# Taking a batched matrix product's last store out of the hand-written section and issuing one load from another engine

One core of a Trainium2 chip runs the kernel. The metric is the device time of one execution in microseconds (us), the median of several; lower is better. Spans, instruction times and DMA packets come from one profiled execution of each kernel.

## The reference

Sixteen products of 512x512 float32 matrices, the second of each transposed:

```python
batch, m, k, n = 16, 512, 512, 512
np.matmul(a, b.transpose(0, 2, 1)).astype(np.float32)   # a: 16x512x512, b: 16x512x512
```

It reads 33.55 MB and writes 16.78 MB.

## The kernel before

The kernel is written by hand, with its own semaphores (counters that one engine or transfer raises and an engine waits for), inside one section of the framework (a block that the framework enters and leaves as a whole, with a handshake of the engines). Inputs come as 16 loads of 2 MB (load 2u holds two matrices of `a`, load 2u+1 two of `b`) into 7 slots; outputs leave as 16 stores of 1 MB. DVE (VectorE) casts a load to bf16, PE (TensorE) transposes and multiplies, ACT (ScalarE) copies the product into one of 7 output slots. SP (SyncE) issues all loads but the second and stores 8 to 15; GpSimd (POOL in the profile) issues stores 0 to 7 and waits for stores to land, which frees the output slots.

```python
STORES = "SSSSOSOSOSSOOOOOO"          # what GpSimd does in turn: S issue a store, O wait for one
LATE = {11: (8, 9), 13: (10, 11), 15: (12, 13)}
# ... (semaphores and buffers cut)
load(0)                                # on SP
load(1, nc.scalar)
for n in range(2, NL):                 # NL = 7: loads 2 to 6, on SP
    load(n)
for n in range(2 * pairs):             # SP: wait for load n, tell DVE, issue load n + 6
    nc.sync.wait_ge(s_ld[n % NL], 16 * (n // NL + 1)).then_inc(s_go, 1)
    if n > 0 and n + NL - 1 < 2 * pairs:
        load(n + NL - 1)
    for m in LATE.get(n, ()):
        store(m)
store(batch - 2)
store(batch - 1)
for n in range(batch - NO, batch - 1): # stores 9 to 14 have landed
    nc.sync.wait_ge(*landed(n))

nc.gpsimd.wait_ge(s_ld[0], 32)         # GpSimd: no store before load 7 is in
for what in STORES:
    ...                                # S: store(n_st);  O: wait for landed(n_of), count s_of up
# ... (DVE, ACT and PE loops cut), then, behind that section, a second one:
with tc.tile_critical(no_gpsimd_drain=True):
    nc.sync.wait_ge(*landed(batch - 1))   # store 15 has landed
```

## Time and profile before

| | before |
|---|---|
| time, median of 3 runs | 125.49 us (125.47 to 125.68) |
| profiled span | 123.5 us |
| DMA engines, mean rate over the span | 407 GB/s |
| PE busy | 90.7 us (73%) |
| landing of the last store to the end of the span | 1.33 us |

The landing is the last of 16 arrivals at the store's semaphore, one from each DMA engine (122.217 us, in a span of 123.549 us). The profile's slices, rates, GpSimd issues and the waits of SP's queue are shown in the prediction below. These are the last two rows of the timeline; the columns are start, length, engine, line, operation, and the number of instructions merged into the row:

```profile
112.38 1.09 ACT L213 COPY ob<-ps 128x512 f32 x2 [0.60 <-PE ps L255]
113.50 0.33 SPq L109 DMA_DIRECT2D out_dram<-ob  x1
```

The last product is copied out at 113.47 us and store 15 is issued at once; nothing computes in the ten microseconds that follow. The DMA engines have a backlog of stores to work off, and then the program has to notice that they are done.

### The profile page before, as it was taken

Reading aid. Unit: us, or ns where it says so; the run is one execution under the profiler, and the core shown is the slowest. Engines: PE = TensorE matmul, PEld = TensorE weight load, DVE = VectorE, ACT = ScalarE, POOL = GpSimd, SP = SyncE. Lnnn points to the kernel's source line nnn. Section 1 sums busy time; section 2 is a strip of 40 time slices with the busy share of each in tenths; the row PEclk is TensorE's granted clock in tenths of the full one; section 3 lists DMA queues with packets and bytes.
Section 4 is the critical chain, followed back from the end, with each engine's and each line's share of the span. In section 5 each row is a group of like instructions: output and inputs, shape, how many; then the busy total and the mean of one; then the engine's idle time right before and its main releaser. Section 6 shows DMA issues by size and latency. Waiting matters only on the chain. (4 is left out here: it accounts for less than half of the span.)

```text
span 123.5 us, 2364 instructions
## 1 busy us (share of the span) xinstructions
PE 90.7 (73%) x768; PEld 55.8 (45%) x768; DVE 67.9 (55%) x96; ACT 68.1 (55%) x130; POOL 5.9 (5%) x14
## 2 busy tenths in 40 slices
PE   0000089999899999989998999899999946994000
PEld 0000079546734774476467447644764535441000
DVE  0000597891898389568928991894787078400000
ACT  4000063458946885595769558937876069555000
POOL 2000000000000160001010230000000000000000
PEclk9999999999999999999999999999999999999955
DMA  4999999999999999999999999999999999999990
GB/s 127 419 446 435 424 424 430 424 424 424 430 430 435 424 403 385 461 390 427 454 400 454 424 414 454 411 432 446 416 438 419 416 427 422 430 424 427 430 385 11
DMA packets 4608, 50.33 MB, mean 407 GB/s; under 512 B 512, under 2 KB 512, under 8 KB 512
## 3 DMA queue, kind: packets, MB, share of 16 engines
q1 hardware_dynamic: 3312, 39.85, 76.2%
q0 software_dynamic: 1152, 8.39, 16.1%
q10 hardware_dynamic: 144, 2.10, 4.3%
HBM read 33.55 MB, written 16.78 MB: 407 GB/s over the span
## 5 line engine op out<-in xcount | busy, mean ns | idle before, releaser
L255 PE MATMUL ps<-tb,ta 128*128 128x512 bf16 x256 | 57.8, 379 | 0.5
L213 ACT COPY ob<-ps 128x512 f32 x64 | 34.5, 588 | 28.5 <-PE ps L255 24.6
L195 ACT COPY ta<-tp 128x512 bf16<-128x512 bf16 x64 | 32.8, 610 | 15.4 <-PE tp L236 15.4
L255 PEld LDWEIGHTS ps<-tb,ta 128*128 128x128 bf16 x256 | 24.1, 97 | 30.7 <-issue 4.0
L236 PE MATMUL tp<-ident,ha 128*128 128x128 bf16 x256 | 19.6, 230 | 19.3 <-PEq L141 19.3
L236 PEld LDWEIGHTS tp<-ident,ha 128*128 128x128 bf16 x256 | 16.6, 103 | 23.1 <-issue 21.3
L176 DVE COPY tb<-tp 128x1024 bf16<-128x1024 bf16 x32 | 21.2, 684 | 4.8 <-DVEq L141 4.8
L236 PE MATMUL tp<-ident,hb 128*128 128x128 bf16 x256 | 18.1, 227 | 2.2 <-PEq L141 2.2
L236 PEld LDWEIGHTS tp<-ident,hb 128*128 128x128 bf16 x256 | 16.1, 102 | 2.6 <-issue 2.6
L160 DVE CAST ha<-ld 128x1024 bf16 x8 | 5.5, 686 | 13.7 <-DVEq L141 13.7
L171 DVE COPY ha<-wa 128x2048 bf16<-128x2048 bf16 x8 | 5.5, 692 | 13.6 <-DVEq L141 13.6
L166 DVE CAST wa<-ld 128x2048 bf16 x8 | 9.8, 1227 | 0.0
L166 DVE CAST wb<-ld 128x2048 bf16 x8 | 9.7, 1218 | 0.0
L160 DVE CAST hb<-ld 128x1024 bf16 x8 | 5.5, 688 | 6.4 <-DVEq L141 6.4
L109 POOL DMA_DIRECT2D out_dram<-ob x8 | 5.2, 655 | 65.2 <-DMA ld<-in_b_dram 41.1
L175 DVE COPY hb<-wb 128x2048 bf16<-128x2048 bf16 x8 | 5.5, 684 | 0.1
L163 DVE CAST ha<-ld 128x1024 bf16 x8 | 5.5, 686 | 0.0
L163 DVE CAST hb<-ld 128x1024 bf16 x8 | 5.5, 683 | 0.0
L186 ACT ACT_TABLE_LOAD x1 | 1.3, 1283 | 1.5 <-SPq L44 1.5
L80 POOL TENSOR_SCALAR_AFFINE_SELECT ident<-ident 128x128 bf16<-128x128 bf16 x1 | 0.3, 282 | 0.2 <-POOL ident L78 0.2
L78 POOL MEMSET ident<- 128x128 bf16 x1 | 0.2, 204 | 0.5 <-SPq L44 0.5
L186 ACT COPY one<-const-float32-1.0 128x1 f32<-128x1 f32 x1 | 0.2, 191 | 0.0
(4 smaller groups left out, 0.4 us busy)
## 6 DMA issues: line engine op xcount, KB each, us to landing
ld<-in_a_dram SPq DMA_DIRECT2D x8, 2048.0 KB, 26.3
ld<-in_b_dram SPq DMA_DIRECT2D x7, 2048.0 KB, 29.8
out_dram<-ob POOLq DMA_DIRECT2D x8, 1024.0 KB, 29.0
out_dram<-ob SPq DMA_DIRECT2D x8, 1024.0 KB, 19.6
ld<-in_b_dram ACTq DMA_DIRECT2D x1, 2048.0 KB, 12.2
```

The costliest lines, as they stand in the source:

```text
L109: engine.dma_start(out[n].rearrange("(p j) n -> p j n", j=J), ob[:, n % NO]).then_inc(landed(n)[0], 16)
L160: nc.vector.tensor_copy(out=h[:, :J, :], in_=src[:, :J, :HK]).then_inc(s_cd, 1)
L163: nc.vector.tensor_copy(out=h[:, J:, :], in_=src[:, J:, :HK]).then_inc(s_c, 1)
L166: nc.vector.tensor_copy(out=w[:], in_=src[:, :, HK:]).then_inc(s_w, 1)
L171: nc.vector.tensor_copy(out=ha[:], in_=wa[:]).then_inc(s_ca, 1)
L175: nc.vector.tensor_copy(out=hb[:], in_=wb[:]).then_inc(s_cb, 1)
L176: nc.vector.tensor_copy(out=tb[:, ko, :], in_=tp[:, 2 + ko % 2].rearrange("k j p -> k (j p)"),).then_inc(s_eb, 1)
L186: nc.scalar.copy(out=one[:], in_=nc.const_aps.tensor(1.0, (P, 1), f32))
L195: c = nc.scalar.copy(out=ta[:, ko, e * J * P:(e + 1) * J * P].rearrange("k (j p h) -> k j p h", j=J, h=2), in_=tp[:, ko % 2, :, e * HP:(e ...
L213: c = nc.scalar.copy(out=dst[:, j, :].rearrange("m (p j) -> m p j", j=2 * J), in_=ps[:, j, :].rearrange("m (j p) -> m p j", j=2 * J),)
L236: t = nc.tensor.transpose(tp[:, 2 * x + g, j, :], h[:, j, g * P:(g + 1) * P], ident[:])
L255: t = nc.tensor.matmul(ps[:, j, :], ta[:, ko, (e * J + j) * P:(e * J + j + 1) * P], tb[:, ko, :].rearrange("k (j p) -> k j p", j=2 * J)[:, ...
```

## The change

It has two parts. The last store leaves the hand-written section: it becomes a plain DMA of the framework behind it, which the framework itself waits for, and the waits for stores 9 to 14 go to ACT, beside that store. The closing section that did nothing but wait is gone from SP's path. And load 6, the seventh, moves from SP to GpSimd, where it waits for load 4 and comes ahead of the stores; it has its own semaphore, so `came(n)` replaces the count of arrivals.

```diff
+        def came(n):
+            if n == NL - 1:
+                return s_sw, 16
+            return s_ld[n % NL], 16 * (n // NL + (n % NL < NL - 1))
...
-        for n in range(2, NL):
+        for n in range(2, NL - 1):
             load(n)
...
         store(batch - 2)
-        store(batch - 1)
-        for n in range(batch - NO, batch - 1):
-            nc.sync.wait_ge(*landed(n))
+        nc.gpsimd.wait_ge(s_ld[NL - 3], 16)
+        load(NL - 1, nc.gpsimd)
         n_st = n_of = 0
         nc.gpsimd.wait_ge(s_ld[0], 32)
...
-    with tc.tile_critical(no_gpsimd_drain=True):
-        nc.sync.wait_ge(*landed(batch - 1))
+    with tc.tile_critical(sync_engine=act, no_gpsimd_drain=True):
+        for n in range(batch - NO, batch - 1):
+            nc.scalar.wait_ge(*landed(n))
+    waits = nc.cur_bb.bb.instructions[-1]
+    last = nc.sync.dma_start(
+        out[batch - 1].rearrange("(p j) n -> p j n", j=J), ob[:, (batch - 1) % NO]
+    )
+    tc.add_manual_dep(last.ins, waits.name, ..., reason="order of issue")   # orders, does not wait
```

(The counts in `landed` follow `came`; cut.)

More of the change, by code (lines that the diff above doesn't have):

```diff
@@ L58 @@
         s_ld = [sem(f"s_ld{i}") for i in range(NL)]
+        s_sw = sem("s_sw")
         s_st = [sem(f"s_st{i}") for i in range(SW)]
@@ L95, in load @@
                 nc.sync.wait_ge(s_cd, n - NL + 2)
-            engine.dma_start(ld[:, slot], src).then_inc(s_ld[slot], 16)
+            engine.dma_start(ld[:, slot], src).then_inc(came(n)[0], 16)
         def landed(n):
@@ L103, in landed @@
             slot = (n - STORES.count("S") + 2) % NL
-            return s_ld[slot], 16 * (len(range(slot, 2 * pairs, NL)) + 1 + (n - STORES.count("S") >= NL))
+            return s_ld[slot], came(2 * pairs - 1 - (2 * pairs - 1 - slot) % NL)[1] + 16 * (
+                1 + (n - STORES.count("S") >= NL)
+            )
         def store(n):
@@ L114 @@
         load(1, nc.scalar)
-        for n in range(2, NL):
+        for n in range(2, NL - 1):
             load(n)
         for n in range(2 * pairs):
-            nc.sync.wait_ge(s_ld[n % NL], 16 * (n // NL + 1)).then_inc(s_go, 1)
+            nc.sync.wait_ge(*came(n)).then_inc(s_go, 1)
             if n > 0 and n + NL - 1 < 2 * pairs:
@@ L265 @@
                                 t.then_inc(s_mm, 1)
-    with tc.tile_critical(no_gpsimd_drain=True):
-        nc.sync.wait_ge(*landed(batch - 1))
+    with tc.tile_critical(sync_engine=act, no_gpsimd_drain=True):
[4 more added lines that the diff above has]
+        out[batch - 1].rearrange("(p j) n -> p j n", j=J), ob[:, (batch - 1) % NO]
+    )
+    tc.add_manual_dep(
+        last.ins,
+        waits.name,
+        mybir.DependencyInfo(mybir.DependencyClass.NoSync, mybir.DependencyReason.DATA),
+        reason="order of issue",
+    )
 _INS = ['a', 'b']
```

## The prediction

> **What bounds the kernel now.** I read the page's slices first, then the DMA queues, the bytes moved by stretch, the waits of SP's queue, and last the instructions of the final 10 us one by one. One core does 16 products of 512x512; 33.55 MB come in and 16.78 MB go out.
>
> ```profile
> PE   0000089999899999989998999899999946994000
> DMA  4999999999999999999999999999999999999990
> GB/s 127 419 446 435 424 424 430 424 424 424 430 430 435 424 403 385 461 390 427 454 400 454 424 414 454 411 432 446 416 438 419 416 427 422 430 424 427 430 385 11
> ```
>
> A digit is a fortieth of the span, 3.09 us. The DMA engines read 9 in every slice from the second to the last but one, while PE starts only in the sixth and stops three slices before the end. So the kernel is bound by moving 50.33 MB at about 428 GB/s, 117.6 us, plus what lies before the first packet and after the last.
>
> ```profile
> core 0: us, PE busy (x) PEld busy (x) DVE busy (x) ACT busy (x) POOL busy (x), PEclk, DMA share, GB/s
> 12.00:42.00 30.00, 25.61 (x211) 16.98 (x212) 21.71 (x30) 16.86 (x33) 0.00 (x0) 1.00 1.01 430
> 42.00:44.00 2.00, 1.52 (x25) 1.22 (x23) 1.77 (x3) 2.00 (x5) 1.19 (x2) 1.00 1.06 451
> 44.00:46.00 2.00, 1.99 (x28) 1.65 (x28) 1.50 (x4) 1.91 (x4) 1.28 (x3) 1.00 1.08 426
> 46.00:48.00 2.00, 1.94 (x10) 0.77 (x9) 2.00 (x4) 0.79 (x2) 0.00 (x0) 1.00 0.92 332
> 48.00:54.00 6.00, 6.00 (x50) 3.53 (x49) 3.45 (x5) 4.12 (x9) 0.00 (x0) 1.00 0.98 418
> 54.00:56.00 2.00, 1.51 (x25) 1.22 (x23) 2.00 (x4) 2.00 (x5) 0.27 (x1) 1.00 1.06 438
> 56.00:96.00 40.00, 38.29 (x328) 22.78 (x326) 29.38 (x42) 28.59 (x55) 2.47 (x4) 1.00 1.01 429
> 114.00:120.00 6.00, 0.00 (x0) 0.00 (x0) 0.00 (x0) 0.00 (x0) 0.00 (x0) 0.79 1.01 427
> 120.00:122.00 2.00, 0.00 (x0) 0.00 (x0) 0.00 (x0) 0.00 (x0) 0.00 (x0) 0.50 0.12 49
> ```
>
> The last column is the rate. It is flat at 427 to 430 with one dent, from 42 to 56 us: 451x2 + 426x2 + 332x2 + 418x6 + 438x2 = 5802 there, where 14 us at 429 would be 6006, so 204/429 = 0.48 us of transfer is lost. The dent sits where GpSimd issues its first DMAs:
>
> ```profile
> 42.81 2.47 POOL L109 DMA_DIRECT2D out_dram<-ob  x4 [41.13 <-DMA ld<-in_b_dram]
> 55.73 0.53 POOL L109 DMA_DIRECT2D out_dram<-ob  x1 [10.45 <-DMA out_dram<-ob]
> ```
>
> In the DMA packets of the trace the loads' 16 KB packets, elsewhere 611 ns each, take 613 to 1099 ns from 45.0 to 47.5 us, and the first packet of GpSimd's queue starts at 47.03, 4.2 us after its issue. The stores issued there at 55.7, 63.0 and 70.4 leave no dent of that size. So it looks like a one-off price of the first use of that queue; whether of the first use, or of four stores issued together, the trace does not tell.
>
> At the end, SP waits:
>
> ```profile
> SPq L127 <- DMA out_dram<-ob: 5.8, 3, 2.4
> SPq L109 <- ACT ob L213: 1.8, 1, 1.8
> SPq L295 <- DMA out_dram<-ob: 1.7, 1, 1.7
> ```
>
> L127 are the waits for stores 9 to 14, L295 is that for store 15. By the instruction records SP issues store 15 at 113.50; the last wait of L127 ends at 119.77; a handshake between the engines takes SP from 119.96 to 120.54; the wait for store 15 ends at 122.24. Its last packet ends at 121.75, though 15 of the 16 DMA engines are done by 120.67 or so: one lags by some 1.2 us. After 122.24 SP goes through a branch (122.28), a semaphore (122.43), a drain (122.52), a no-op (122.59) and two drains (122.63 and 122.70); then two barriers of all engines end the span at 123.55.
>
> **What the Trainium skill says.** "DMA: Bandwidth & Descriptors", section "Issuing engines are not separate DMA queues", says that DMAs from scalar, sync and gpsimd run on the same 16 engines and interleave, so another issuer only saves issue time. The trace agrees: with two queues active from 56 to 96 us the rate is 429, with one from 12 to 42 us it is 430. The same page, "Anatomy of one DMA — SWDGE (gpsimd) path", gives about 2 us of fixed cost to a GpSimd DMA, most of it completion; here first issue to first packet alone took 4.2 us. "SBUF — State Buffer" says in its trap "DVE blocks DMA" that GpSimd cannot write descriptors while VectorE runs a two-port operation; VectorE is busy 1.77 of the 2 us from 42 to 44, which fits a slow start, but no run here shows the cause. On the cost of a critical section's exit I found no page.
>
> **The change part by part.**
>
> (a) The waits for stores 9 to 14 move to ACT, in a second section; store 15 becomes a plain DMA after the first section, and the framework itself waits for it. In the built program SP has, between that last wait and the first closing barrier, only one drain. So what stood before the barrier's drain, from the branch at 122.28 to the drain at 122.63, falls away: 122.634 - 122.277 = 0.36 us, on the path that sets the end. The handshake of 119.96 to 120.54 also leaves SP, but it lay beside store 15's transfer: worth nothing. ACT's own waits end with store 14, about 119.8, and its leave-taking about 0.5 us later, well before 122.2.
>
> (b) Store 15 is issued later: after ACT's last copy ends (112.89 + 0.59 = 113.47) and the handshake of the first section, which took SP 0.38 us in the kernel before (119.96 to 120.35). I estimate 113.9 instead of 113.50. Store 14 lands from 117.99 on, so store 15 need not be ready earlier; with 1.9 us from an SP issue to its first packet (0.95 to 2.84 us, the first load) there are still about 2 us to spare. Cost: 0.
>
> (c) Load 6 leaves SP's queue and waits on GpSimd for load 4, which lands at 27.8. With the 4.2 us seen above its packets start at about 32, when load 5 lands (32.0 to 32.7). Then it shares the engines half and half with load 7, which SP issued at 16.8. Both are 2 MB, so both land near 42.5: load 6 five us later than before (36.9 to 37.6), load 7 as before. VectorE casts load 6 at 46.42, so nothing waits for it. SP stands longer in its wait for load 6, but the load that it issues next needs that same cast and goes out at 47.13 either way. Bytes and packets stay equal. Cost: 0.
>
> (d) The dent moves from 45 us to about 30 us, and the first stores start at about 45 instead of 47. If the dent is a price of first use it is paid once either way: 0. In a transfer-bound stretch an earlier store only displaces a load.
>
> Sum: -0.36 us. The median of 125.49 becomes 125.13; as two of the earlier runs lie under it and a smaller dent is about as likely as a second one, I put 125.1.
>
> **Rivals.** First, the dent vanishes: a load alone on a quiet GpSimd queue may start softer than four stores in 2.47 us. For it: only that burst shows a dent. Against: 16 engines have to take up the new queue in any case. It would give 125.13 - 0.48 = 124.65. Second, both pay: if the burst is the cause, the four stores dent at 45 us again and the load adds its own, between 0.1 (a quarter of the burst) and 0.48 us: 125.2 to 125.6, eating the gain. Third, the lag of the one engine changes. Among the arrivals of one transfer on 16 engines, first to last takes 0.69 us while only SP loads, 1.1 us once GpSimd's stores mix in (load 8), 1.74 us for the last store. If GpSimd's queue causes it, 2 MB more on it beside its 8.39 MB could add 0.2 to 0.3 us; if not, nothing. Fourth, compute becomes the bound: load 6 later by more than 9 us (37.6 to 46.4) would stall PE, and then the last store would slip. The DMA share of 1.01 speaks against it, since nothing makes the two loads together later than 43 us. It would cost up to a few us, and I give it one in thirty.
>
> **Range and chances.** The sure part is -0.36. The dent adds between -0.48 and +0.48, the lag perhaps ±0.3, the spread of one kernel's runs is 0.2. So 124.5 to 125.6 should hold it 8 times in 10. A gain of 2% means under 122.98, more than all idle transfer time that I can find (dent 0.48, lag 1.2, exit 0.36); a loss of 2% means over 128.0, which only the fourth rival reaches.
>
> **What would show it.** (a) From the end of the wait for store 15 to the end of the span: 0.95 us rather than 1.31. (b) SP's last issue at about 113.9, and its packets with no gap before them. (c) Load 6 landing near 42 us, VectorE's cast still at about 46.4. (d) One dent, near 30 us, of about 0.48 us, and none at 45. The prediction is wrong if the exit stays at 1.3 us, if there are two dents or none, if the last arrival of store 15 moves by over 0.5 us for another reason, or if PE stands idle between pairs 2 and 3.

## The result

The changed kernel took 125.19 us (median of 6 runs, 125.07 to 125.32), the kernel before 125.48 us in the same rounds (125.31 to 125.68). The ratio is 0.9977, 95% interval 0.9964 to 0.999: faster by about a quarter of a percent, and within the 2% that counts as the same. A ratio here is always the mean time of one kernel's fast runs over that of the other's in the same rounds, so it is not quite the ratio of the medians that are quoted.

The slices of the changed kernel, as before: PE, the DMA engines' busy tenths, and the rate.

```profile
PE   0000078999899999989998999899999929997000
DMA  4999999999999999999999999999999999999990
GB/s 122 409 436 436 436 430 425 430 425 430 425 430 430 425 436 404 417 409 441 422 412 433 422 433 444 406 430 444 409 444 425 420 430 425 425 425 425 428 404 19
```

The bound is the same: the DMA engines are full from the second slice to the last but one. Next the busy times by stretch; the last column is the rate in GB/s.

```profile
28.00:30.00 2.00, 2.00 (x22) 1.36 (x21) 0.00 (x0) 1.40 (x4) 0.68 (x1) 1.00 1.02 434
30.00:32.00 2.00, 1.69 (x28) 1.37 (x25) 1.61 (x3) 2.00 (x5) 0.00 (x0) 1.00 0.98 418
32.00:34.00 2.00, 1.83 (x27) 1.62 (x28) 1.51 (x4) 2.00 (x5) 0.00 (x0) 1.00 1.00 426
42.00:44.00 2.00, 1.51 (x25) 1.22 (x23) 2.00 (x4) 2.00 (x5) 0.86 (x2) 1.00 1.02 434
44.00:46.00 2.00, 2.00 (x27) 1.41 (x23) 1.51 (x3) 1.59 (x4) 1.48 (x3) 1.00 1.02 434
46.00:48.00 2.00, 1.94 (x10) 0.81 (x9) 2.00 (x4) 1.07 (x2) 0.00 (x0) 1.00 0.92 344
```

The dent of the kernel before is still at 46 to 48 us (344 against 332), and where load 6 opens GpSimd's queue, at 30 to 34 us, there is none. These are GpSimd's first two rows of DMA issues, SP's last issue, and VectorE's first cast of load 6:

```profile
28.46 0.68 POOL L103 DMA_DIRECT2D ld<-in_a_dram  x1 [26.78 <-DMA ld<-in_a_dram]
43.14 2.34 POOL L118 DMA_DIRECT2D out_dram<-ob  x4 [14.01 <-DMA ld<-in_b_dram]
```

```profile
114.23 0.33 SPq L282 DMA_DIRECT2D out_dram<-ob  x1
```

```profile
46.09 0.68 DVE L169 CAST ha<-ld 128x1024 bf16 x1
```

Load 6 is issued at 28.46 us instead of 3.46; its first packet starts at 32.34, 3.9 us later, and it has landed on all 16 engines at 43.31 (37.62 before). VectorE casts it at 46.09, as before (46.42). And the waits of SP's queue (SPq) from 113.4 us on:

```profile
SPq L316 <- DMA out_dram<-ob: 7.7, 1, 7.7
SPq L316 <- PEq L316: 0.8, 2, 0.6
SPq L44 <- ACTq L44: 0.7, 1, 0.7
```

The three waits for stores on L127 are no longer SP's; one wait of 7.7 us, for store 15, is left. The instruction records around it, SP alone, put the two exits side by side (start in us; a wait is given from the end of the instruction before it):

```
before                                        after
120.541  wait for store 15, till 122.239      114.629  wait for store 15, till 122.395
122.277  branch                               122.439  drain
122.432  semaphore                            122.499  drain of the first closing barrier
122.517  drain                                123.376  end of the span
122.590  no-op
122.634  drain
122.698  drain of the first closing barrier
123.549  end of the span
```

From the end of the wait to the barrier's drain it is 0.459 us before and 0.104 after. From the last arrival of store 15 to the end of the span it is 1.332 us before and 1.026 after (122.350 to 123.376), a gain of 0.31 us. The profiled span shrank by less, 123.549 to 123.376, because the last arrival came 0.13 us later in that execution.

### The profile page after: what moved, and what is told of

Read it like the earlier page. It is cut to its first block, busy times and chain, and to the rows that moved or that the text cites. A ratio compares the mean times of both kernels' runs of the same rounds, so it can differ in the third digit from the quotient of the medians.

```text
span 123.4 us, 2365 instructions
## 1 busy us (share of the span) xinstructions
PE 91.1 (74%) x768; PEld 56.0 (45%) x768; DVE 68.0 (55%) x96; ACT 68.2 (55%) x130; POOL 6.4 (5%) x15
## 5 line engine op out<-in xcount | busy, mean ns | idle before, releaser
L103 POOL DMA_DIRECT2D ld<-in_a_dram x1 | 0.7, 675 | 26.8 <-DMA ld<-in_a_dram 26.8
```

## The experiments

Two theories were to be told apart. The first: the whole gain is the shorter exit and the load's move is worth nothing. Its rival: the load's move helps or hurts by itself, through the dent in the rate or through the one DMA engine that ends last. And the dent's cause was open, since the prediction had put it to the first use of GpSimd's queue. All outputs are right.

**The kernel before, profiled again**

No edit but a comment.

> The kernel before, profiled a second time, to see what of a profile repeats. If the dent in the transfer rate between 42 and 56 us belongs to the program, it is there again with a loss of 0.4 to 0.55 us and the largest drop again at 44 to 48 us; if it is an accident of one execution, it moves or changes by half. The spread of the arrivals of the last store over the 16 DMA engines was 1.77 us before and 1.87 after the change: if that difference of 0.1 means nothing, this run lies anywhere from 1.6 to 2.0.

One run, 125.52 us. The dent is there again. To measure it more finely than by whole packets, I spread the bytes of each DMA packet in the trace evenly over its time and add up what 42 to 56 us lack of 430 GB/s: 0.55 us in the first profile of the kernel before, 0.44 us in this one. (The views count each packet whole, in one stretch; they gave the 0.48 us of the prediction.) The arrivals of store 15 spread over 1.82 us, against 1.77 before and 1.87 after the change. So both belong to the program, and differences of 0.1 us in either mean nothing.

**The exit alone**

```diff
 # the kernel before, with the second section and the last store as in the change; load 6 stays on SP
-        store(batch - 1)
-        for n in range(batch - NO, batch - 1):
-            nc.sync.wait_ge(*landed(n))
...
+    with tc.tile_critical(sync_engine=act, no_gpsimd_drain=True): ...
+    last = nc.sync.dma_start(...)
```

> Only the first part of the change: store 15 as a plain DMA with the waits on ACT, load 6 left on SP's queue. Theory: the whole gain is the shorter exit, so this is 0.3 to 0.36 us faster than the kernel before (ratio 0.9971 to 0.9977), and from the end of the wait for store 15 to the end of the span takes 0.98 us as in the changed kernel and not 1.31. Rival: the load's move gives part of the gain; then this gains under 0.2 us.

125.09 us (5 runs, 124.96 to 125.25) against 125.44: ratio 0.9971 (0.9957 to 0.9985), 0.35 us. SP's waits at the end are those of the changed kernel, one wait for the store:

```profile
SPq L303 <- DMA out_dram<-ob: 7.9, 1, 7.9
```

From the last arrival to the end of the span took 1.00 us. The exit gives the whole gain.

**The load alone**

```diff
 # the changed kernel with the old end
+        store(batch - 1)
+        for n in range(batch - NO, batch - 1):
+            nc.sync.wait_ge(*landed(n))
...
+    with tc.tile_critical(no_gpsimd_drain=True):
+        nc.sync.wait_ge(*landed(batch - 1))
```

> Only the second part: load 6 on GpSimd's queue, the old exit kept. Theory: nothing, ratio 0.999 to 1.001, with the dent at 44 to 48 us still there and none near 30 us. Rival one (the load has a price in the lag of one engine): 0.1 to 0.2 us slower. Rival two (the load brings part of the gain): 0.1 us or more faster.

125.47 us (5 runs, 125.40 to 125.59) against 125.44: ratio 1.0006 (0.9992 to 1.002). Nothing, within the interval. The stretch of the dent reads:

```profile
46.00:48.00 2.00, 1.94 (x10) 0.82 (x10) 2.00 (x4) 1.07 (x2) 0.00 (x0) 1.00 0.87 311
```

It stayed although GpSimd's queue had been in use since 28.4 us. The exit takes the old 1.34 us.

**The closing section twice**

```diff
     with tc.tile_critical(no_gpsimd_drain=True):
         nc.sync.wait_ge(*landed(batch - 1))
+    with tc.tile_critical(no_gpsimd_drain=True):
+        nc.sync.wait_ge(*landed(batch - 1))
```

> The kernel before with its closing section, which waits for store 15, written twice; the second wait is met at once. If a section on SP behind the last store costs what the profile shows, the end comes later by at least the 0.36 us of one more branch, semaphore, drain and no-op, and by up to about 0.6 us more if the engines' handshake (0.58 us in the first exit) is repeated: 0.36 to 0.95 us slower, ratio 1.003 to 1.0075. If the exit's instructions are hidden beside something else, no change.

126.29 us (4 runs, 126.13 to 126.46): ratio 1.0074 (1.0059 to 1.009), 0.85 us slower. In the records the second pass runs from SP's branch at 122.156 to the next at 122.803, 0.65 us, with a handshake of no-op and three waits that are all met at once; the last arrival to the end of the span is 1.98 us against 1.33. The other 0.2 us of the measured loss I could not place. So an empty section behind the last store is not hidden beside anything, and the direction of the theory is confirmed from the other side.

**The first store alone**

```diff
-    STORES = "SSSSOSOSOSSOOOOOO"
+    STORES = "SOSSSOSSOSSOOOOOO"
```

> The kernel before, but GpSimd issues store 0 alone and the next three only when it has landed. The dent in the rate near 44 to 48 us did not move with load 6, so it is not a price of the first use of GpSimd's queue. Theory (burst): four stores issued together make it; then it is gone at 44 to 48 us, or under 0.15 us, and a dent of 0.2 to 0.4 us follows where the next three are issued, near 55 us. Rival (first writes): the first store of all makes it, whatever follows; then 0.3 to 0.5 us are lost at 44 to 48 us as before, and nothing near 55.

One run, 125.58 us. The stretches around the first store (42.79 us) and around the next three (55.89 us):

```profile
46.00:48.00 2.00, 2.00 (x10) 0.88 (x10) 2.00 (x3) 1.07 (x2) 0.00 (x0) 1.00 0.95 348
54.00:56.00 2.00, 1.81 (x30) 1.67 (x31) 1.50 (x4) 2.00 (x5) 0.11 (x1) 1.00 1.01 430
56.00:58.00 2.00, 1.94 (x14) 0.83 (x11) 2.00 (x4) 0.71 (x3) 1.46 (x3) 1.00 1.07 459
```

One store makes the dent (0.49 us between 42 and 56), and three together make none: the loss against 430 GB/s is 0.01 us between 56 and 66. The burst theory falls. The packets show more: store 0's end at 54.8 us and the next store's start at 59.6, so the loads ran alone for 4.8 us, and these stores each write a new matrix. Neither brought a second dent.

**The stores as early as they are ready**

```diff
-        nc.gpsimd.wait_ge(s_ld[0], 32)
```

> The kernel before without GpSimd's wait for load 7, so each store is issued when its product is ready: store 0 near 28 us, stores 1 to 3 one by one after it. Burst theory: no dent at all, 0.2 to 0.4 us less transfer time, ratio 0.997 to 0.999, unless a later load makes the tensor engine wait. First-writes rival: a dent of 0.3 to 0.5 us near 30 us in place of the one at 46, ratio 0.999 to 1.001. Loads land later here, so a compute wait between pairs can add up to 1 us in either theory; then PE shows idle time before 60 us.

126.19 us (4 runs, 125.83 to 126.26): ratio 1.0049 (1.0033 to 1.0065), 0.75 us slower. The dent came along with the stores (0.55 us between 28 and 42, and 0.02 between 42 and 56); but the loss is elsewhere, at the end:

```profile
30.00:32.00 2.00, 1.68 (x28) 1.36 (x25) 1.62 (x3) 2.00 (x5) 0.82 (x1) 1.00 1.06 377
32.00:34.00 2.00, 1.83 (x27) 1.62 (x28) 1.50 (x4) 2.00 (x5) 0.00 (x0) 1.00 0.90 348
114.00:116.00 2.00, 2.00 (x11) 0.88 (x9) 0.00 (x0) 1.09 (x2) 0.00 (x0) 1.00 0.70 295
116.00:118.00 2.00, 2.00 (x10) 0.78 (x8) 0.00 (x0) 1.25 (x3) 0.00 (x0) 1.00 0.31 131
```

Early stores delay the loads, PE stalls and finishes late, and the DMA engines run dry at 114 to 118 us, where 2.0 us of transfer are lost. In PE's timeline the stalls stand in brackets:

```profile
79.86 1.86 PE L235 MATMUL tp<-ident,hb 128*128 128x128 bf16 x16 [2.89 <-PEq L140]
94.36 1.05 PE L235 MATMUL tp<-ident,hb 128*128 128x128 bf16 x16 [2.32 <-PEq L140]
```

The compute wait lies later than I had expected (before 60 us). So GpSimd's wait for load 7 is worth keeping: loads have to run ahead of stores here. And one thing more: here, where the engines came to rest shortly before, the arrivals of the last store spread over 0.17 us, not the 1.6 to 2.3 of every other profile. As the whole loss is only 0.75 us, the lag seems to have been worked off in the idle stretch.

**No DMA on GpSimd**

```diff
-    STORES = "SSSSOSOSOSSOOOOOO"
-    SW = 5                            # semaphores for these stores
+    STORES = "OOOOOOOOO"              # GpSimd only waits
+    NS = 8                            # stores 0 to 7: issued by ACT
+    SW = 8
-        nc.gpsimd.wait_ge(s_ld[0], 32)
...
-        with nc.Fori(0, pairs, engines=[act]) as u:
+        for u in range(pairs):
...                                    # after the four copies to ta:
+            for n in (2 * u - 2, 2 * u - 1):
+                if 0 <= n < NS:
+                    store(n)
```

A first form of this kernel and of the next one, with the five store semaphores kept, was refused before the chip: GpSimd's wait on a semaphore could have been met by either of two stores. Besides the issuer the edit moves the stores' time: without the wait for load 7 they start some 10 us earlier.

> The kernel before with no DMA on GpSimd at all: stores 0 to 7 are issued by ACT in its unrolled loop, two per product pair from about 30 us on; GpSimd only waits for them to land. If GpSimd's queue makes the dent and the lag of the last DMA engines, both go: no stretch under 420 GB/s between 30 and 100 us, the arrivals of the last store spread over under 1.0 us and not 1.7 to 1.9, ratio 0.990 to 0.994 (0.75 to 1.2 us). If the dent comes from mixing reads with the first writes and the lag from the engines themselves, both stay and the ratio is 0.998 to 1.002. A loss would mean that ACT, held by issuing, delays the products.

126.14 us (5 runs, 125.96 to 126.15): ratio 1.0048 (1.0035 to 1.0061), slower, where I had expected a gain or nothing. There is no GpSimd DMA, and the dent is there, now at the first stores from ACT:

```profile
34.00:36.00 2.00, 1.94 (x10) 0.71 (x8) 2.00 (x4) 0.90 (x3) 0.00 (x0) 1.00 1.12 369
36.00:38.00 2.00, 2.00 (x11) 0.91 (x10) 2.00 (x3) 1.32 (x3) 0.00 (x0) 1.00 0.86 336
```

The arrivals of store 15 spread over 2.30 us. So neither the dent nor the lag is GpSimd's. The first store's packets began at 36.84 us, 4.0 us after ACT had issued it at 32.84, about as long as from GpSimd. The products do end 2.9 us later than before (last copy to 116.36 us instead of 113.47), but the rate from 96 to 120 us is 427 GB/s, as before (bytes spread), so that delay is not what cost the time. In this one profile the dent is larger (0.74 us between 28 and 42, against 0.55 and 0.44 for the kernel before, between 42 and 56) and the last arrival comes at 122.99 us instead of 122.22; what made it so is not settled. Nor is it settled whether the issuer or the earlier start counts.

**The same with the short exit**

The edit of the exit and of the stores on ACT together.

> The run with stores 0 to 7 on ACT, plus the short exit that gained 0.35 us alone. The two act at different places, so their gains add: 0.30 to 0.40 us faster than the run with ACT's stores. If the exit's gain needed the lag (ACT's waits run while the last engine finishes), it shrinks to under 0.2 us.

125.49 us (6 runs, 125.23 to 125.84): ratio to the kernel before 1.0008 (0.9992 to 1.0025), and 0.65 us under the run without the exit's part, more than the 0.30 to 0.40 expected. The last arrival to the end of the span took 1.02 us, against 1.34 without: 0.32 us, as everywhere. The other third of a microsecond is in the transfers: spread 1.79 us against 2.30, and a dent of 0.50 us against 0.74. Why, I do not know. These profiles are of the fastest run here (125.23 us; the runs scatter from there to 125.84) and of the slowest one without the exit's part (126.15), so a part of their difference can be chance.

**Exit alone beside the whole change**

> The exit-only kernel once more, beside the whole change in the same rounds: 0.30 to 0.40 us faster than the kernel before. If the load's move is worth nothing, the two lie within 0.1 us of each other; if it costs something by itself, this one is 0.1 us or more faster than the whole change.

> The whole change once more: 0.25 to 0.40 us faster than the kernel before, within 0.1 us of the exit alone. In the profile the dent is at 44 to 48 us again and none near 30.

Exit alone: 125.09 us (4 runs, 125.02 to 125.17), ratio 0.9969 (0.9955 to 0.9983). Whole change: 125.29 us (4 runs, 125.03 to 125.47), ratio 0.998 (0.9965 to 0.9995). Over all rounds the exit alone has a median of 125.09 us (9 runs), the whole change 125.195 (10 runs). That is 0.1 us for the simpler kernel, with overlapping ranges (124.96 to 125.25, 125.03 to 125.47), so the load's move costs between nothing and about 0.2 us. By the test set beforehand (0.1 us or more) the 0.20 us of these rounds speak for a cost, and both expectations for the whole change, 0.25 to 0.40 us and within 0.1 us of the exit alone, were missed. The load's move alone showed no loss (1.0006), but its interval, up to 1.002, admits 0.25 us. So this stays undecided. If it costs something, the profiles do not show where: the spread of the last arrivals is 1.74, 1.87 and 2.08 us in the three profiles with load 6 on GpSimd, and 1.61, 1.77, 1.82, 1.89 and 1.92 us in the five of the kernel before, the exit alone and the section twice. The dent does not tell them apart either (0.46, 0.35 and 0.46 us against 0.45, 0.55, 0.44, 0.33 and 0.41). One small difference is in the records: GpSimd's clearing of the semaphores in the final barrier takes 243 ns in the two profiles of the whole change, which has one semaphore more, and 226 in the two of the exit alone. (With the old exit the same semaphore moved it from 223 to 225 ns only.)

**A small write, early**

```diff
 # the exit-only kernel and, behind load 1 on ACT:
+        nc.scalar.dma_start(
+            out[batch - 1].rearrange("(p j) n -> p j n", j=J)[:, 0, :P], early[:]
+        ).then_inc(s_w1, 16)
```

> The exit-only kernel, plus one 64 KB write to the last output matrix, issued by ACT behind load 1, so that it moves near 13 us, long before the first store (its zeros are overwritten by store 15). The dent came with the first stores in every run, whatever queue they were on (44 to 48 us from GpSimd, 34 to 38 us from ACT). If the very first write of the program makes it, the dent moves to about 13 us or vanishes, and the time is 0.3 to 0.5 us below the exit alone. If it comes each time that a sustained stream of writes joins the loads, or when new stretches of the output are first written, it stays at 44 to 48 us with 0.3 to 0.5 us lost, and the time is that of the exit alone plus 0.1 to 0.15 us for the 64 KB.

125.40 us (4 runs, 125.32 to 125.51), 0.31 us over the exit alone in the same rounds, more than the 0.15 that its bytes explain; the rest is open. The dent stays where it was, 0.53 us between 42 and 56:

```profile
46.00:48.00 2.00, 1.94 (x10) 0.91 (x10) 2.00 (x3) 1.07 (x2) 0.00 (x0) 1.00 1.02 360
```

**A large write, early**

The same with 1 MB, from an output slot that GpSimd has zeroed.

> The exit-only kernel, plus a whole 1 MB write to the last output matrix, issued by ACT behind load 1, so near 13 to 18 us (zeros, overwritten by store 15). The 64 KB write left the dent where it was. If a dent comes with the first sustained stream of writes and then no more, 0.3 to 0.5 us are lost at 13 to 18 us and nothing at 44 to 48. If it comes each time that a stream of stores joins the loads, there is one at 13 to 18 and one at 44 to 48 us. If it comes with the first writes to each new stretch of the output, the same two, so this run does not tell those apart. The 1 MB itself costs 2.45 us, so the time is 127.5 us or a little more, unless the later loads delay the products.

One run, 127.98 us against 125.50. There are two dents, one at the early write and one at the first real stores (issued at 46.05 us here):

```profile
10.00:12.00 2.00, 0.00 (x0) 0.00 (x0) 0.00 (x0) 0.00 (x0) 0.00 (x0) 1.00 1.04 344
12.00:14.00 2.00, 0.00 (x0) 0.00 (x0) 0.00 (x0) 0.00 (x0) 0.00 (x0) 1.00 0.90 344
48.00:50.00 2.00, 2.00 (x11) 0.92 (x10) 2.00 (x3) 1.41 (x3) 1.09 (x1) 1.00 1.07 393
50.00:52.00 2.00, 2.00 (x11) 0.94 (x10) 1.32 (x2) 1.12 (x3) 0.00 (x0) 1.00 0.93 393
```

Spread as before, they are worth 0.7 us and 0.3 us. So it is not paid once for a program. Two explanations offer themselves: it comes when stores join loads that were running alone, or when a part of the output is first written. Neither holds in its plain form. In the run with the first store alone, stores joined loads that had run alone for 4.8 us, without a dent; here the loads had run alone for 29 us (20.96 to 50.28). And in the kernel before, stores 1 to 5, each to a matrix not yet written, land between 56 and 96 us, where only 0.05 us is lost in all. A longer time without stores, or a larger region of the output, would fit both runs; no run here tells these apart.

## Why the prediction was right

The time, 125.1 us forecast, was 125.19, inside 124.5 to 125.6.

(a) The exit: 0.36 us was read from the records of the kernel before, and it is right for the part it described (0.459 to 0.104 us between the wait and the barrier's drain, 0.355). From the end of the wait to the end of the span it is 0.98 us, where 0.95 was forecast. From the last arrival to the end of the span the gain is 0.31 to 0.33 us in the profiles, since the new wait ends 0.045 us after the arrival instead of 0.022 and the semaphores' clearing grew by 0.003 to 0.02 us. It repeats: 1.33 or 1.34 us with the old exit in six profiles, 1.00 to 1.03 us with the new one in seven. Timed alone it gave 0.35 us twice. The handshake of 0.58 us that also left SP's path was worth nothing, as forecast.

(b) The later issue of store 15: forecast 113.9, measured 114.23, because the products ended 0.57 us later in that execution. The handshake was overrated: from the end of ACT's last copy to the issue took 0.18 us, not about 0.4; the two errors partly cancel. In two other profiles it was 114.99 and 115.07 us. It cost nothing each time; the DMA engines stayed full (share 1.01 from 114 to 120 us in all three).

(c) Load 6: issue, first packets (32 forecast, 32.34 measured), landing (42.5 forecast, 43.31 on the last engine) and VectorE's cast were as forecast, and the load's part timed alone was 1.0006. That it costs 0.1 us is possible and not shown. The slow start is not bound to what the prediction set beside it, GpSimd's queue and VectorE's operations: a store from ACT took 4.0 us from issue to first packet, and load 6, issued on GpSimd while VectorE did nothing (0.00 us busy from 28 to 30), took 3.9.

(d) Here a step failed: that the dent "looks like a one-off price of the first use of that queue" and moves to about 30 us, with the first stores at about 45. It stayed at 46 to 48 us, and the first store's packets came at 47.15, 4.0 us after the issue at 43.14 (4.2 in the kernel before), although GpSimd's queue had been used. One store alone makes it, three together do not, stores from ACT make it where they start, and a megabyte written early makes one more. It goes with the start of the stores beside running loads, and in one run again after a long time without stores, not with an issuer; its cause is open. The sum came out unharmed only because the dent stayed one dent of about the same size, which was the zero that I had entered for another reason.

Of the rivals, the first (the dent vanishes), the second (both pay) and the fourth (compute stalls) did not happen. For the third, the lag of one engine, no effect of GpSimd's queue is visible, and without any GpSimd DMA the lag was as long (1.79 and 2.30 us). The prediction's reading that it is 0.69 us "while only SP loads" differs from execution to execution: for load 2, before any of the sixteen stores, the spread is 0.61 to 1.13 us in different profiles, 1.08 in one of the exit alone. (Its 1.74 us for the last store is that of the store before; the last one has 1.77.) In the kernel before it grows from 0.69 us (load 7) to 1.11 (load 8, beside the first store) and 1.77 at the end; with the stores on ACT it grew alike, from 0.93 to 2.30. What makes one engine late stays open; where the engines had idled it was 0.17 us.

## What to carry to other kernels

When transfers fill the span, look for time to win before the first packet and after the last arrival: list what the issuing engine still executes after the last arrival. Here it paid 0.35 us to let the framework wait for the last store instead of a section of one's own. Which engine issued one load was worth about 0.2 us at most, and stores that went out before the loads that compute needed cost 0.75 us. A dent in the rate is not explained by what happens to stand above it in the profile: move one suspect, then another, before you name it.

## What the Trainium skill lacked or had wrong

- "DMA: Bandwidth & Descriptors", "Issuing engines are not separate DMA queues", holds: load 6 from GpSimd instead of SP gave a ratio of 1.0006. But the page says nothing of a loss when the first stores start beside running loads, which was 0.3 to 0.7 us of transfer time in every profile here, from GpSimd and from ACT.
- The same page, "Latency and other measured facts", gives about 0.6 us to the first byte for DMAs from SP and ACT and about 1 us from GpSimd. With the DMA engines full, issue to first packet took 4.0 us from ACT (a store), 4.2 us from GpSimd (a store) and 3.9 us from GpSimd (a load).
- The same section guesses that some DMA engines are slow because of GpSimd's descriptor rings. In the two kernels without any GpSimd DMA the last engine's arrival still came 1.2 and 1.5 us after the one before it, and in the others 1.0 to 1.5 us, but for the run whose engines had idled. (The trace kept here does not say which engine it was.)
- No page gives the cost of ending a program behind a section of one's own: 0.31 to 0.33 us for the one removed here, 0.65 us in the records (0.85 us timed) for one more.
